# A 32-byte gap in on-chip memory ahead of the weights' pool of a two-layer hybrid encoder kernel

## The chip, the cores and the metric

The kernel runs on one core of a Trainium2 chip. The metric is the device time of one launch in microseconds (us). The kernel before takes 981.59 us, the median of three runs (981.29 to 983.07). Inside a core, TensorE multiplies matrices, VectorE (DVE), ScalarE (ACT) and GpSimd (POOL) do elementwise work, and SyncE (SP), among others, issues transfers (DMA). All of them read operands from a memory of 128 partitions (SBUF). A tile has the same byte address in each of its partitions, and this address is what the change moves.

## The reference

The kernel computes two layers of a bidirectional encoder for 256 positions and 2048 channels. Cut to what matters:

```python
for i in range(DEPTH):                       # DEPTH = 2
    hn = _rmsnorm(h, norm_g[i])
    u = hn @ w_in[i]                         # 2048 x 5632
    a_val, a_glu, a_z, q, k, v, b_z = jnp.split(u, offs, axis=-1)
    ya = _conformer_conv(a_val, a_glu, conv_w[i], conv_b[i], cln_g[i], cln_b[i])
    ya = ya * jax.nn.silu(a_z)
    yb = _window_attention(q, k, v, bias_band, sink[i]) * jax.nn.silu(b_z)
    h = h + jnp.concatenate([ya, yb], axis=-1) @ w_out[i]
    e = _rmsnorm(p[i] @ w_pe[i], pe_g[i])    # 256 x 2048
    h = h + e * jax.nn.sigmoid(h @ w_pg[i])
return _rmsnorm(h, final_g)
```

Everything is 32-bit floating point. Nearly all of the arithmetic lies in the products with `w_in`, `w_out`, `w_pg` and `w_pe`.

## The kernel before

**The products.** Activations lie transposed: channels on the partitions, the 256 positions along the free axis. A product has a block of weights of 128 x 128 as the stationary operand, which TensorE loads first (a weight load, PEld in the profile), and a block of activations, 128 x 256, as the moving operand, which then streams through (PE). To keep precision at a faster matmul type (`float32r`), each operand is split into a high and a low part, and a product is made of three: high times high, high times low, low times high. `mm3` does this in one of two forms. The narrow form (lines 402, 403, 404) issues three matmuls of 256 columns, each with its own weight load. The wide form (lines 399, 400) issues one matmul of 512 columns (high weights against the high and the low activations side by side), and one of 256 columns (low weights against the high activations), so two weight loads for the same 768 columns. The wide form is used for `w_pg` (tiles `g`) and half of `w_out` (tiles `o` with operand `ya`); the narrow one for everything else.

**The weights.** They arrive in transfers of 1 MB (tiles `raw`, pool `wraw`, three buffers), each holding two halves of 128 x 1024. For each half, `split` writes a tile `w` of pool `wspl` (five buffers): ScalarE casts the high part (line 166), VectorE subtracts it from the raw values for the low part (line 169). A half serves eight products. `get` and `ahead` make the split run up to four halves ahead of TensorE. The order on TensorE, VectorE and ScalarE is that in which the program is written: the scheduler is off for these three. Convolution steps on VectorE (line 577) are fed in between from a queue, a few for each half.

**Stages.** In each layer: `e` (`w_pe`), `ag` (convolution inputs), `k`, `v`, `zb` and `q` with attention in between, `za`, `o` (output projection), `g` (gate). In layer 0, `e` is made from `raw` without a split (line 499); in layer 1, it uses `w` against a small tile `pp`.

**Where the tiles lie.** Pools are laid out one behind the other in the order in which they are opened, and each tile takes a multiple of 32 bytes. The five pools of SBUF start at these byte addresses (in every partition), and the last column is the address modulo 64:

| pool, what it holds | size | start before | mod 64 |
|---|---|---|---|
| `big`: `hg`, `ya`, `yb`, `h` and other operands and sums | 5 x 16384 | 16512 | 0 |
| `wraw`: `raw` | 3 x 8192 | 98432 | 0 |
| `wspl`: `w` | 5 x 8192 | 123008 | 0 |
| `cst`: gains, parameters, `ident`, `ones`, then `mhalf` | 12064 | 163968 | 0 |
| ... of these, `keys` and all behind `mhalf` | | | 32 |
| `wk`: `pp`, `qq`, `sq`, `hn`, `s`, `ptt`, `v` and other working tiles | | 176032 | 32 |

`mhalf` needs 8 bytes and takes 32; hence what follows it, the whole pool `wk` except a few tiles of some bytes among it, lies half a line of 64 bytes off. Inside the tiles, the weight blocks of 128 columns lie 512 bytes apart, and the activations' blocks 1024, so that a matmul's operands start where their tile starts, modulo 64. So before the change `w` and the operands `hg`, `ya`, `yb`, `h` agree modulo 64, and three kinds of matmul have other pairs: `e` of layer 1 (moving `pp` at 32, weights `w` at 0), the attention scores `sc` (moving `keys` at 32, weights `qq` at 32), and the matmuls that multiply unsplit f32.

Of the kernel before, what the change touches and what calls it, by code (L numbers as in the profile page):

```python
# [10 lines left out]
F32 = mybir.dt.float32  # L11
# [6 lines left out]
P = 128  # L18
# [110 lines left out]
def trunk_kernel(ctx: ExitStack, tc: tile.TileContext, xT, pT, wst, par, gain, relb, sinkp, onehot, out):  # L129
    nc = tc.nc  # L130
# [2 lines left out]
        ctx.enter_context(tc.manual_schedule(engines={getattr(ET, x) for x in MAN.split(",")}))  # L133
    big = ctx.enter_context(tc.tile_pool(name="big", bufs=5))
    wraw = ctx.enter_context(tc.tile_pool(name="wraw", bufs=3))
    wspl = ctx.enter_context(tc.tile_pool(name="wspl", bufs=NSPL))
    cst = ctx.enter_context(tc.tile_pool(name="cst", bufs=1))
    wk = ctx.enter_context(tc.tile_pool(name="wk", bufs=2))
# [805 lines left out]
```

## Time and profile before

| what | value |
|---|---|
| median of three runs | 981.59 us |
| the profiled execution's span, first to last instruction | 978.2 us |
| mean granted TensorE clock | 0.997 |
| matmuls, weight loads | 7216, 7216 |
| HBM read and written, over the span | 185 GB/s |

The page gives no time of the profiled execution but its span, which is 3.4 us less than the median of the three runs. How to read it: PE is a matmul in flight and PEld a weight load in flight. Matmuls overlap, since one starts before the one ahead of it has left the array, so the busy share of PE says little. What tells the rate is the distance from the start of one matmul to the start of the next. A row of the timeline has a start, a duration, the engine, the source line, the operation, and output<-moving,stationary by the program's names.

### The profile page before, as it was taken

The page shows a single profiled execution, that of the slowest core. Times are in us where ns is not written, and L with a number is a line of the kernel's source. Part 1 is how long each engine was busy: PE and PEld are TensorE (multiplying, and loading weights), DVE is VectorE, ACT ScalarE, POOL GpSimd, SP SyncE. Part 2 cuts the span into 40 slices and gives each one's busy share as a digit, 9 for nine tenths or more (in the row PEclk, how much of TensorE's full clock was granted, in tenths as well). Part 3 has the DMA queues.
Part 4 walks back from the last instruction along what each step waited for, and adds up shares of the span by engine and source line. Part 5 has one row for each costly group of instructions (what it writes and reads, how often), then busy time and mean ns, then how long its engine had stood idle before and what let it go on. Part 6 is the DMA issues. An engine that isn't in the chain of part 4 may idle for free.

```text
span 978.2 us, 17740 instructions
## 1 busy us (share of the span) xinstructions
PE 965.9 (99%) x7216; PEld 914.6 (93%) x7216; DVE 793.7 (81%) x1369; ACT 557.9 (57%) x861; POOL 84.3 (9%) x79
## 2 busy tenths in 40 slices
PE   9999999999999999999999999999999999999996
PEld 7999999999999998888899999999999999888885
DVE  4899989987787777787789998988887878677763
ACT  4655455777774544555566444468787545446652
POOL 0022001010000000011103200000100000000111
PEclk9999999999999999999999999999999999999998
DMA  7664636555547454656546565565444555545532
GB/s 291 227 233 172 216 129 237 187 180 178 173 150 245 141 209 172 211 173 224 205 174 216 173 214 175 172 210 193 158 162 172 172 196 183 186 167 196 177 125 86
DMA packets 29005, 182.45 MB, mean 187 GB/s; under 512 B 3595, under 2 KB 4156, under 8 KB 9084
## 3 DMA queue, kind: packets, MB, share of 16 engines
q1 hardware_dynamic: 24284, 165.70, 48.6%
q0 software_dynamic: 3344, 12.88, 4.0%
q10 hardware_dynamic: 1296, 2.75, 0.8%
q8 instruction: 56, 0.92, 0.4%
q14 instruction: 25, 0.20, 0.1%
HBM read 177.09 MB, written 4.23 MB: 185 GB/s over the span
## 4 chain that ended last, share of the span: by engine, by line
PE 96%; DVE 2%; DMA 1%; ACT 0%; issue 0%; ACTq 0%; DVEq 0%
PE g L399 12%; PE o L399 6%; PE ag L404 6%; PE ag L402 6%; PE ag L403 6%; PE g L400 6%; PE za L402 3%; PE zb L402 3%; PE q L402 3%; PE o L402 3%; PE o L403 3%; PE o L404 3%; PE zb L403 3%; PE q L403 3%; PE za L403 3%; PE zb L404 3%
## 5 line engine op out<-in xcount | busy, mean ns | idle before, releaser
L169 DVE TENSOR_TENSOR w<-raw,w 128x1024 fp32r<-128x1024 f32 x306 | 372.3, 1226 | 104.9 <-ACT w L166 99.8
L166 ACT CAST w<-raw 128x1024 fp32r<-128x1024 f32 x308 | 314.2, 1046 | 161.2 <-PE ag L404 43.5
L577 DVE SCALAR_TENSOR_TENSOR cz<-az,pars,cz 128x241 f32<-128x241 f32 (+11 forms) x480 | 217.9, 503 | 1.9 <-ACT cz L570 0.9
L399 PE MATMUL g<-h,w 128*128 128x512 f32 x496 | 175.3, 399 | 0.0
L404 PE MATMUL ag<-hg,w 128*128 128x256 f32 x512 | 145.1, 283 | 0.5 <-DVE w L169 0.5
L402 PE MATMUL ag<-hg,w 128*128 128x256 f32 x512 | 145.4, 284 | 0.0
L403 PE MATMUL ag<-hg,w 128*128 128x256 f32 x512 | 145.0, 283 | 0.0
L400 PE MATMUL g<-h,w 128*128 128x256 f32 x496 | 139.3, 281 | 0.0
L399 PEld LDWEIGHTS g<-h,w 128*128 128x128 f32 x496 | 93.2, 188 | 23.2
L402 PEld LDWEIGHTS ag<-hg,w 128*128 128x128 f32 x512 | 97.5, 191 | 0.9 <-ACT cz L570 0.8
L404 PEld LDWEIGHTS ag<-hg,w 128*128 128x128 f32 x512 | 97.5, 191 | 0.8 <-DVE w L169 0.7
L403 PEld LDWEIGHTS ag<-hg,w 128*128 128x128 f32 x512 | 97.6, 191 | 0.1
L400 PEld LDWEIGHTS g<-h,w 128*128 128x128 f32 x496 | 93.7, 189 | 0.0
L399 PE MATMUL o<-ya,w 128*128 128x512 f32 x256 | 90.5, 399 | 0.0
L402 PE MATMUL za<-hg,w 128*128 128x256 f32 x256 | 73.7, 288 | 0.0
L402 PE MATMUL q<-hg,w 128*128 128x256 f32 x256 | 73.3, 286 | 0.0
L402 PE MATMUL zb<-hg,w 128*128 128x256 f32 x256 | 73.1, 286 | 0.0
L402 PE MATMUL o<-yb,w 128*128 128x256 f32 x256 | 73.1, 286 | 0.0
L403 PE MATMUL o<-yb,w 128*128 128x256 f32 x256 | 72.6, 283 | 0.0
L403 PE MATMUL zb<-hg,w 128*128 128x256 f32 x256 | 72.4, 283 | 0.0
L404 PE MATMUL o<-yb,w 128*128 128x256 f32 x256 | 72.4, 283 | 0.0
L403 PE MATMUL q<-hg,w 128*128 128x256 f32 x256 | 72.4, 283 | 0.0
(224 smaller groups left out, 2094.3 us busy)
## 6 DMA issues: line engine op xcount, KB each, us to landing
raw<-in_wst SPq DMA_DIRECT2D x153, 1024.0 KB, 4.9
bias<-fscr POOLq DMA_DIRECT2D x16, 384.0 KB, 3.7
raw<-in_wst SPq DMA_DIRECT2D x4, 512.0 KB, 8.1
az<-in_xT POOLq DMA_DIRECT2D x4, 512.0 KB, 6.0
hscr<-e POOLq DMA_DIRECT2D x2, 1024.0 KB, 5.0
az<-hscr POOLq DMA_DIRECT2D x4, 512.0 KB, 5.8
x<-in_xT SPq DMA_DIRECT2D x3, 512.0 KB, 8.3
out_t<-og ACTq DMA_DIRECT2D x4, 256.0 KB, 3.3
```

Of the source, the lines that this page charges most:

```text
L166: nc.scalar.copy(hi, raw)
L169: nc.vector.tensor_sub(lo, raw, hi.bitcast(F32))
L399: nc.tensor.matmul(o, w[:, 0], x, start=start, stop=False, skip_group_check=True)
L400: nc.tensor.matmul(o[:, 1], w[:, 1], x[:, 0], start=False, stop=stop, skip_group_check=True)
L402: nc.tensor.matmul(o, w[:, 0], x[:, 0], start=start, stop=False, skip_group_check=True)
L403: nc.tensor.matmul(o, w[:, 0], x[:, 1], start=False, stop=False, skip_group_check=True)
L404: nc.tensor.matmul(o, w[:, 1], x[:, 0], start=False, stop=stop, skip_group_check=True)
L577: nc.vector.scalar_tensor_tensor(acc[:, t, lo_:hi_], a[:, t, lo_ + s:hi_ + s], w(k), acc[:, t, lo_:hi_], ALU.mult, ALU.add)
```

## The change

A pool of one tile of 32 bytes is opened between `wraw` and `wspl`, and VectorE sets it to zero once.

```diff
     big = ctx.enter_context(tc.tile_pool(name="big", bufs=5))
     wraw = ctx.enter_context(tc.tile_pool(name="wraw", bufs=3))
+    gap = ctx.enter_context(tc.tile_pool(name="gap", bufs=1))
+    nc.vector.memset(gap.tile([P, 8], F32, name="gap"), 0.0)
     wspl = ctx.enter_context(tc.tile_pool(name="wspl", bufs=NSPL))
     cst = ctx.enter_context(tc.tile_pool(name="cst", bufs=1))
     wk = ctx.enter_context(tc.tile_pool(name="wk", bufs=2))
```

The addresses after it: `big` and `raw` stay. `w` starts at 123040, 32 modulo 64. The first part of `cst` is at 32, `keys` at 0, and `wk` starts at 176064, 0 modulo 64. So `w` differs by half a line from `hg`, `ya`, `yb`, `h`, and from `pp` too, with the sides exchanged (weights at 32, moving at 0). `qq` and `keys` agree as before, now at 0.

Of the instructions, one is added, and none is moved. At the program's start, VectorE's rows before were these (`zeros` is what the warming matmuls read, `relt` holds the bias table):

```order
L256 MEMSET zeros 128x256
L305 MEMSET ones 128x128
L307 MEMSET mhalf 128x2
L310 MEMSET relt 1x16
L389 TENSOR_TENSOR hacc<-hacc,sq 128x512 x6
```

and the same place of the changed kernel, where source lines stand two further down, has the row of the gap ahead of them:

```order
L137 MEMSET gap 128x8
L258 MEMSET zeros 128x256
L307 MEMSET ones 128x128
L309 MEMSET mhalf 128x2
L312 MEMSET relt 1x16
L391 TENSOR_TENSOR hacc<-hacc,sq 128x512 x6
```

Only this memset has moved the others down by one place. The rows of the other engines are the same ones in the same order.

## The prediction

> **What bounds the kernel now.** I read the page's shares first, then the chain of work that ended last, then TensorE's waits.
>
> ```profile
> PE 965.9 (99%) x7216; PEld 914.6 (93%) x7216; DVE 793.7 (81%) x1369; ACT 557.9 (57%) x861; POOL 84.3 (9%) x79
> ...
> PEclk9999999999999999999999999999999999999998
> ...
> PE 96%; DVE 2%; DMA 1%; ACT 0%; issue 0%; ACTq 0%; DVEq 0%
> ...
> PE rh0c L352 <- DVE fold L376: 1.2, 1, 1.2
> PE warm L259 <- DVE zeros L256: 1.2, 1, 1.2
> PE ag L404 <- DVE w L169: 0.5, 1, 0.5
> PE rfc L352 <- ACT sq L812: 0.4, 1, 0.4
> ```
>
> TensorE makes 96% of the chain, its granted clock is full, and by the last four rows (total, times, longest) it waits for other engines 3.3 us in all. Thus the span is the number of matmuls times the distance from one start to the next, and only what changes this distance moves the time. I take the distance from timeline rows. The first pair is the narrow form on `w` and `hg`, both at 0 modulo 64; the second is `e` of layer 1, the same form and the same engine order, with `w` at 0 and `pp` at 32.
>
> ```profile
> 299.78 0.28 PE L402 MATMUL za<-hg,w 128*128 128x256 f32 x1
> ...
> 301.94 0.28 PE L402 MATMUL za<-hg,w 128*128 128x256 f32 x1
> ...
> 497.51 0.28 PE L404 MATMUL e<-pp,w 128*128 128x256 f32 x1
> ...
> 501.38 0.28 PE L404 MATMUL e<-pp,w 128*128 128x256 f32 x1
> ```
>
> Between the first two lie 18 starts: 2.16 us / 18 = 120.0 ns. Between the other two lie 33: 3.87 / 33 = 117.3 ns. The groups by form say the same over all matmuls of these kinds, in their mean durations, and they add the weight loads:
>
> ```profile
> L404 PE MATMUL v<-w,hg 128*128 128x256 f32 x64 | 18.1, 283 | 0.0
> L403 PE MATMUL e<-pp,w 128*128 128x256 f32 x32 | 9.0, 280 | 0.0
> ...
> L404 PEld LDWEIGHTS za<-hg,w x256: 187/192/192, 249.2 to 779.6; 128*128 128x128 f32 x128
> L404 PEld LDWEIGHTS e<-pp,w x32: 187/188/192, 489.0 to 501.3; 128*128 128x128 f32 x32
> ```
>
> A matmul takes 283 ns where the two operands agree modulo 64 and 280 where they differ by half a line; in `v` the sides are exchanged (weights `hg`, moving `w`), and it is 283 all the same. A load's median is 192 ns and 188 ns (minimum/median/maximum). So the kernel before holds an example of what the change makes of all its products, and there a narrow matmul is 120.0 - 117.3 = 2.7 ns shorter.
>
> **The change, part by part.** *How many matmuls.* Seven rows of the groups on the page carry the counts:
>
> ```profile
> L399 PE MATMUL g<-h,w 128*128 128x512 f32 x496 | 175.3, 399 | 0.0
> L404 PE MATMUL ag<-hg,w 128*128 128x256 f32 x512 | 145.1, 283 | 0.5 <-DVE w L169 0.5
> L399 PE MATMUL o<-ya,w 128*128 128x512 f32 x256 | 90.5, 399 | 0.0
> L402 PE MATMUL za<-hg,w 128*128 128x256 f32 x256 | 73.7, 288 | 0.0
> L402 PE MATMUL q<-hg,w 128*128 128x256 f32 x256 | 73.3, 286 | 0.0
> L402 PE MATMUL zb<-hg,w 128*128 128x256 f32 x256 | 73.1, 286 | 0.0
> L402 PE MATMUL o<-yb,w 128*128 128x256 f32 x256 | 73.1, 286 | 0.0
> ...
> L402 PE MATMUL k<-hg,w 128*128 128x256 f32 x64 | 18.2, 284 | 0.0
> ...
> L402 PE MATMUL g<-h,w 128*128 128x256 f32 x16 | 4.5, 283 | 0.0
> ```
>
> Each line of the narrow form stands for three (402, 403, 404): 3 x (512 + 4 x 256 + 2 x 64 for `k` and `v` + 16) = 5040. The wide form has 496 + 256 = 752 pairs. At 120 ns the narrow ones are 604.8 us of the span.
>
> *Narrow form:* 5040 x 2.7 ns = 13.6 us, less what is not at 120 today. Behind each interruption some matmuls come closer together:
>
> ```profile
> 171.02 0.28 PE L645 MATMUL sc<-keys0h,qq 128*128 128x256 f32 x1
> ...
> 171.97 0.28 PE L402 MATMUL zb<-hg,w 128*128 128x256 f32 x1
> ...
> 172.32 0.28 PE L402 MATMUL zb<-hg,w 128*128 128x256 f32 x1
> ```
>
> After the scores (`sc`, eight of them in 0.95 us, 118.8 ns each), three `zb` take 0.35 us, 117 ns each, where `zb` is otherwise at 120. I estimate some 60 interruptions (48 of them by attention: scores, transposes and products for 16 pairs of heads), with some six such matmuls each, that have about 2 ns less to give: 0.7 us. The narrow form gives 12.9 us.
>
> *Wide form.* No row shows it with operands half a line apart; this is the unknown cost. Today three pairs take 1.06 us, 353.3 ns each:
>
> ```profile
> 419.98 0.40 PE L399 MATMUL g<-h,w 128*128 128x512 f32 x1
> 420.21 0.28 PE L400 MATMUL g<-h,w 128*128 128x256 f32 x1
> ...
> 421.04 0.40 PE L399 MATMUL g<-h,w 128*128 128x512 f32 x1
> ```
>
> Say that 256 columns cost c and a load that runs beside them s. Narrow, c + s = 120.0; wide, 3c + 2s = 353.3. So c = 113.3 ns and s = 6.7 ns. By this split `e` pays 4.0 ns for a load where its neighbours pay 6.7. I take the same 2.7 ns off each load, since `e` is the nearest row: 752 x 2 x 2.7 = 4.1 us. The ends are nothing at all, and a load that costs nothing, 752 x 2 x 6.7 = 10.1 us. A loss is not excluded either; it is a rival below.
>
> *The memset.* It stands ahead of `zeros` on VectorE, which the warming matmuls wait for.
>
> ```profile
> 0.86 0.27 DVE L256 MEMSET zeros<- 128x256 f32 x1 [0.86 <-PEq L933]
> ...
> 1.23 0.06 DVE L307 MEMSET mhalf<- 128x2 f32 x1
> ...
> 1.66 8.80 DMA x<-in_xT
> ```
>
> A memset of that size (`mhalf`) takes 0.06 us. The chain starts with the transfer of `x` (last row), so 0.06 us is hidden beneath 8.80 us; without that cover it would cost 0.06.
>
> *VectorE and ScalarE.* They write `w`, and most of their working tiles move by 32 bytes. Rows of the same operation and shape with different pairs before the change:
>
> ```profile
> L475 DVE TENSOR_TENSOR hg<-hn,hg 128x512 fp32r<-128x512 f32 x16 | 11.0, 686 | 0.5
> ...
> L806 DVE TENSOR_TENSOR e<-e,sg 128x512 f32<-128x512 f32 x14 | 9.7, 693 | 1.9 <-ACT sg L804 1.3
> ...
> L756 DVE TENSOR_TENSOR yb<-az,yb 128x512 fp32r<-128x512 f32 x8 | 5.2, 686 | 2.2 <-ACT yb L755 2.2
> ...
> L389 DVE TENSOR_TENSOR vacc<-vacc,sq 128x512 f32<-128x512 f32 x6 | 4.2, 692 | 4.3 <-ACT sq L388 4.3
> ```
>
> `yb` has all at 0 (686 ns), `hg` reads one at 32 (686), `e` reads one at 32 (693), `vacc` has all at 32 (692). No order by address: I cost this at nothing.
>
> *Is the weights' split fast enough?* VectorE is full in one stage. The first row is a stretch of the run with the busy time of PE, PEld, VectorE and ScalarE (and the instructions); the second is VectorE on line 169 alone, the third PE and PEld on line 404 alone, from other stretches.
>
> ```profile
> 60.00:120.00 60.00, 60.00 (x503) 60.00 (x502) 59.63 (x96) 28.39 (x36) 13.24 (x9) 1.00 0.57 193
> ...
> 0.00:95.00 95.00, 30.70 (x25) 1.00 0.67 237
> ...
> 24.00:95.00 71.00, 54.16 (x191) 36.63 (x191) 1.00 0.62 217
> ```
>
> In 60 to 120 us VectorE is busy 59.63 us, and TensorE waits all the same nowhere in it, since the split runs ahead. By 95 us, line 169 has run 25 times (second row), and line 174 twice: 27 halves; TensorE has started 191 third products (line 404, third row), eight a half, 23.9 halves. The lead is three halves or 3 x 24 x 120 ns = 8.6 us. TensorE faster by 2.2% eats 71 x 2.2% = 1.6 us of it by then. The cover holds. At the start of the first `ag`, where the wait of 0.5 us is, some tenths may come back: 0.3 us.
>
> **Sum:** 12.9 + 4.1 - 0.3 = 16.7 us off the span of 978.2, so 961.5. With the 3.4 us by which the median of the runs lies above this span, 981.6 - 16.7 = 964.9, say **965 us**, 1.7% less.
>
> One rule speaks against all of it. The Trainium skill, page "SBUF — State Buffer", section "SBUF: two separate sides", says that TensorE never waits for another user of the memory, and its section "A bandwidth-pool intuition that's wrong (but worth ruling out)" gives the weight load a second, independent read port. By that rule, a load and a stream could not disturb each other by their addresses, and the time would stay; 117.3 beside 120.0 ns is a first row against it.
>
> **The rivals.**
>
> *It does nothing.* The shorter distance in `e` could come from `pp` itself: it starts at 32, or lies far from `hg`, and its high and low parts are 2 KB apart where those of `hg` are 8 KB apart. Then `w` at 32 changes nothing; only `v`, whose moving operand is now `w` at 32, would gain 192 x 2.7 ns = 0.5 us, and `e` would lose 96 x 2.7 = 0.3. For it: the scores have both operands at 32, agree modulo 64, and still have 118.8 ns, not 120. Against it: they are only eight at a time, and behind an interruption `zb` shows such distances with both at 0. Time: 981.4, within 0.2%. The rule of the Trainium skill above ends here too.
>
> *Weights that begin in mid-line cost more (slower).* 512 bytes from a start at 0 are eight lines of 64; from 32 they touch nine. If what a load costs goes by its lines, and not by its relation to the stream, each load goes from 6.7 to 6.7 x 9/8 = 7.5 ns: 0.83 x (5040 + 1504) = 5.4 us, 987 us. It decides wherever the ninth line costs more than the half line saves. For it: no example has weights at 32 with a long run; `e` has the moving operand there. Against it: `qq` is a weight at 32, and the scores are not above 120.
>
> *The loads become free (much faster).* 6544 x 6.7 ns = 43.8 us, 938 us. For it is only that no conflict would be left in a simple picture of two half lines; `e`, which pays 4.0 ns for its loads, speaks against it.
>
> *Narrow only:* the wide form keeps 353.3 ns: 965 + 4.1 = 969, inside the forecast's own range.
>
> **How the numbers follow.** The forecast, 955 to 972 us, has a chance of 0.62; its upper end is a narrow form that gains only three quarters, with the wide unchanged, its lower end a free load in the wide form and some more in the narrow. Faster still, below 952: 0.05. A smaller gain, 972 to 979: 0.08. Nothing (a difference within 0.2%, about what a measurement of this kernel can tell from no change): 0.14. Slower: 0.11. So faster is 0.62 + 0.05 + 0.08 = 0.75, same 0.14, slower 0.11. The range that leaves out only the slower case and the loads that become nearly free reaches from 952 to 982.
>
> **What would show it.** Right: `za`, `zb`, `q`, `ag` at 280 ns a matmul and 188 a load instead of 283 and 192, eighteen starts in 2.11 us instead of 2.16; `g` with three pairs in about 1.044 instead of 1.06; `e` of layer 1 still at 117.3; VectorE's groups above with the same means; TensorE's waits still some 3 us. Wrong: 283 throughout with `v` alone at 280 (it was the moving operand's own start); 284 and more with `v` at 280 (weights in mid-line); distances that fall while TensorE's waits on `w` grow by as much (the split bounds); or a granted clock below 0.99.

## The result, and the profile after

The changed kernel takes 972.96 us (median of four runs, 972.3 to 973.9) beside 981.44 us of the kernel before. The ratio is 0.9914, with a 95% interval of 0.9899 to 0.9928. The gain is 8.5 us, where 16.7 were forecast: the sign and the place were right, and half of the size is missing. The time lies 1 us above the forecast range of 955 to 972 us, in the band of 972 to 979 that had been given a chance of 0.08.

The page of the changed kernel, with busy times, granted clock and the chain's shares:

```profile
PE 958.8 (99%) x7216; PEld 906.8 (93%) x7216; DVE 793.8 (82%) x1370; ACT 558.9 (57%) x861; POOL 81.0 (8%) x79
...
PEclk9999999999999999999999999999999999999999
...
PE 96%; DVE 2%; DMA 1%; ACT 0%; issue 0%; ACTq 0%; DVEq 0%
```

The shares are those of before: TensorE still sets the time. Its distances are read as before, from rows of the timeline a known number of starts apart. The first two rows are the narrow form, 30 starts apart; the other two are the wide form, twelve pairs apart:

```profile
296.67 0.28 PE L406 MATMUL za<-hg,w 128*128 128x256 f32 x1
...
300.21 0.28 PE L406 MATMUL za<-hg,w 128*128 128x256 f32 x1
...
403.44 0.40 PE L401 MATMUL g<-h,w 128*128 128x512 f32 x1
...
407.68 0.40 PE L401 MATMUL g<-h,w 128*128 128x512 f32 x1
```

Narrow: 3.54 us / 30 = 118.0 ns by these rounded rows (118.2 from the unrounded starts of the trace, which also give the later means; other stretches of 30 have up to 118.5). Wide: 4.24 us / 12 = 353.3 ns a pair. So the narrow form lost 1.8 of its 120.0 ns where 2.7 were expected, and the wide form lost nothing. The groups of loads and matmuls, with minimum/median/maximum in ns:

```profile
L406 PEld LDWEIGHTS za<-hg,w x256: 187/188/192, 248.2 to 774.0; 128*128 128x128 f32 x128
L406 PE MATMUL za<-hg,w x256: 276/280/288, 248.3 to 774.1; 128*128 128x256 f32 x128
L406 PEld LDWEIGHTS v<-w,hg x64: 187/188/189, 131.3 to 613.6; 128*128 128x128 f32 x64
L406 PE MATMUL v<-w,hg x64: 274/279/281, 131.4 to 613.7; 128*128 128x256 f32 x64
```

These medians, 188 and 280, are exactly the forecast's sign of success, and still the distance is not 117.3. The signs that were distances did not appear: eighteen narrow starts take 2.13 us (2.11 forecast), and three wide pairs still take 1.06 us (1.044 forecast). Before the change, the starts were evenly 120 ns apart. Now they repeat in an uneven pattern (116, 116, 120, 117, 122 and so on), and the durations that the profile gives have the same median, 280 ns, at this distance and in `e` before the change, at 117.3. The sign was badly chosen: a distance over many starts is safe, a median is not.

Where the 8.5 us came from is seen by taking the same work in both runs, from about the first `ag` matmul to the end, in stretches of the run (engines: PE, PEld, DVE, ACT, POOL). The first row is of the kernel before:

```profile
24.00:978.20 954.20, 944.29 (x7125) 896.21 (x7123) 783.96 (x1351) 546.89 (x844) 82.86 (x72) 1.00 0.53 184
```

and this is the changed kernel:

```profile
26.00:972.10 946.10, 936.20 (x7124) 888.07 (x7122) 783.72 (x1350) 547.80 (x844) 79.56 (x72) 1.00 0.53 185
```

The same number of matmuls but one takes 954.2 us before and 946.1 now: 8.1 us less, which is 5040 narrow matmuls times 1.6 ns (the mean over all of them fell from 119.9 to 118.3). The work of VectorE and ScalarE did not shrink or grow. The spans of the two profiled executions differ by 6.1 us only, since the changed one lost some 2 us in its first 26 us: there the granted clock was 0.79 between 17 and 25 us, and eight `e` matmuls took nearly twice as long, 3.62 us beside 1.97 before.

```profile
18.34 3.62 PE L501 MATMUL e<-p,raw 128*128 128x256 f32 x8
...
17.00:25.00 8.00, 8.00 (x37) 6.94 (x38) 3.90 (x6) 4.27 (x7) 0.70 (x1) 0.79 0.45 163
```

This dip is not of the change: another execution of the changed kernel has a mean clock of 0.998 and a span of 970.5 us, the profiled one 0.996 and 972.1; and a variant that is as slow as the kernel before (a gap of 256 bytes, below) has the dip too.

TensorE's waits on `w` did not grow. All its waits together went from 3.3 to 4.2 us (total, times, longest), by a later `rh0c` and a wait of `e` on a transfer, both in the first 17 us:

```profile
PE rh0c L354 <- DVE fold L378: 1.7, 1, 1.7
PE warm L261 <- DVE zeros L258: 1.2, 1, 1.2
PE ag L406 <- DVE w L171: 0.5, 1, 0.5
PE e L501 <- DMA raw<-in_wst: 0.4, 1, 0.4
PE rfc L354 <- ACT sq L814: 0.4, 1, 0.4
```

### The profile page after: what moved, and what is told of

Its sections match the earlier page's. It is cut to its first block, busy times and chain, and to the rows that moved or that the text cites. A ratio compares the mean times of both kernels' runs of the same rounds, so it can differ in the third digit from the quotient of the medians.

```text
span 972.1 us, 17741 instructions
## 1 busy us (share of the span) xinstructions
PE 958.8 (99%) x7216; PEld 906.8 (93%) x7216; DVE 793.8 (82%) x1370; ACT 558.9 (57%) x861; POOL 81.0 (8%) x79
## 4 chain that ended last, share of the span: by engine, by line
PE 96%; DVE 2%; DMA 1%; ACT 0%; issue 0%; ACTq 0%; DVEq 0%
PE g L401 12%; PE o L401 6%; PE g L402 6%; PE ag L406 6%; PE ag L404 6%; PE ag L405 6%; PE za L404 3%; PE q L404 3%; PE zb L404 3%; PE o L404 3%; PE o L402 3%; PE o L405 3%; PE o L406 3%; PE za L405 3%; PE q L405 3%; PE zb L405 3%
## 5 line engine op out<-in xcount | busy, mean ns | idle before, releaser
L171 DVE TENSOR_TENSOR w<-raw,w 128x1024 fp32r<-128x1024 f32 x306 | 374.0, 1232 | 101.1 <-ACT w L168 95.5
L406 PEld LDWEIGHTS ag<-hg,w 128*128 128x128 f32 x512 | 96.5, 188 | 0.9 <-DVE w L171 0.9
L404 PEld LDWEIGHTS ag<-hg,w 128*128 128x128 f32 x512 | 96.5, 188 | 0.9 <-ACT w L168 0.8
L405 PEld LDWEIGHTS ag<-hg,w 128*128 128x128 f32 x512 | 96.5, 188 | 0.1
L404 PE MATMUL zb<-hg,w 128*128 128x256 f32 x256 | 72.6, 284 | 0.0
L402 PE MATMUL o<-ya,w 128*128 128x256 f32 x256 | 72.1, 281 | 0.0
```

What stands on the lines that cost most here:

```text
L171: nc.vector.tensor_sub(lo, raw, hi.bitcast(F32))
L402: nc.tensor.matmul(o[:, 1], w[:, 1], x[:, 0], start=False, stop=stop, skip_group_check=True)
L404: nc.tensor.matmul(o, w[:, 0], x[:, 0], start=start, stop=False, skip_group_check=True)
L405: nc.tensor.matmul(o, w[:, 0], x[:, 1], start=False, stop=False, skip_group_check=True)
L406: nc.tensor.matmul(o, w[:, 1], x[:, 0], start=False, stop=stop, skip_group_check=True)
```

## The experiments

Most of them move tiles by gaps made like the one of the change: a pool of one tile, set to zero once. The last two, `lo64` and `mixed`, also move parts inside the tiles `w`. Everything else stays. It will help to have one name: **d**, the start of the weights (the stationary operand) minus the start of the moving operand. Blocks of weights lie 512 bytes apart and blocks of activations 1024, so d is the same for all products of a kind modulo 512 (in `lo64` and `mixed`, modulo 256).

**Relation or own start.** The first four kernels ask whether the two operands' relation counts or each one's own start, whether the shift of the other tiles has a part, and whether a gap as such does anything.

`x32` moves the operands and leaves `w` at its remainder modulo 64:

```diff
+    gap_big = ctx.enter_context(tc.tile_pool(name="gap_big", bufs=1))
+    nc.vector.memset(gap_big.tile([P, 8], F32, name="gap_big"), 0.0)
     big = ctx.enter_context(tc.tile_pool(name="big", bufs=5))
+    gap_wraw = ctx.enter_context(tc.tile_pool(name="gap_wraw", bufs=1))
+    nc.vector.memset(gap_wraw.tile([P, 8], F32, name="gap_wraw"), 0.0)
     wraw = ctx.enter_context(tc.tile_pool(name="wraw", bufs=3))
```

> Operands hg, ya, yb, h (pool big) moved to 32 modulo 64; w, raw, cst and wk keep the remainders of the kernel before. Theory R, only the relation of the two addresses counts: narrow matmuls as in the change, 118.2 ns apart, wide pairs 353.2; about 973 us. Theory S, each operand's own start counts, the moving one's more: narrow 116.7 to 117.3 ns as v and e have it with the moving operand at 32, v itself 118.2; 966 to 969 us if the wide form gains nothing, less if it does.

Measured: 973.69 us, ratio 0.9923 (0.9911 to 0.9935). Its narrow form:

```profile
296.65 0.28 PE L408 MATMUL za<-hg,w 128*128 128x256 f32 x1
...
300.19 0.28 PE L408 MATMUL za<-hg,w 128*128 128x256 f32 x1
```

3.54 us / 30 again, as in the change: the number of theory R.

`w32_x32` has four gaps of 32 bytes, ahead of `big`, `wraw`, `wspl` and `cst`:

> Both w and the operands of pool big at 32 modulo 64, all else with the remainders of the kernel before. Theory R: they agree again, narrow 120 ns, 981 us as before. Theory S: both gains add up, narrow some 115 ns, below 965 us.

Measured: 961.65 us, ratio 0.9811 (0.9792 to 0.9829). This is far from the 981 of theory R, and would fit theory S, had `x32` not spoken against it. Its narrow form comes down to this (30 starts):

```profile
291.69 0.28 PE L412 MATMUL za<-hg,w 128*128 128x256 f32 x1
...
295.09 0.28 PE L412 MATMUL za<-hg,w 128*128 128x256 f32 x1
```

3.40 us / 30 = 113.3 ns; other stretches have 117.8.

`w32_only` is the change with one more gap of 32 bytes, ahead of `cst`:

> The change with a second gap of 32 bytes behind the weights' pool, so that cst and wk keep the remainders of the kernel before and w alone differs. If the operands of the products make the whole gain: narrow 118.2 ns, 973 us. If the shift of the working tiles has a part in it: nearer to 981 us.

Measured: 972.7 us, ratio 0.9923 (0.9911 to 0.9936), narrow 118.2 ns. The working tiles are back at their old remainders modulo 64 (though 64 bytes further on), and the gain stays: their shift by half of that had no part that shows.

`gap64` has one gap, of 64 bytes, where the change has 32:

```diff
-    nc.vector.memset(gap.tile([P, 8], F32, name="gap"), 0.0)
+    nc.vector.memset(gap.tile([P, 16], F32, name="gap"), 0.0)
```

> A gap of 64 bytes in place of 32 ahead of the weights' pool: all remainders modulo 64 as before. Theories R and S: narrow 120 ns, 981 us. If the absolute place or the distance of the pools counts, or the added memset: another time.

Measured: 961.35 us, ratio 0.9798 (0.9784 to 0.9812). Both theories fall: all remainders modulo 64 are those of the slow kernel, and it is the fastest of the four. Its timeline has the narrow form at two distances. The first two rows are 30 starts apart, the second two as well:

```profile
153.82 0.28 PE L406 MATMUL q<-hg,w 128*128 128x256 f32 x1
...
157.22 0.28 PE L406 MATMUL q<-hg,w 128*128 128x256 f32 x1
...
289.76 0.28 PE L406 MATMUL za<-hg,w 128*128 128x256 f32 x1
...
293.30 0.28 PE L406 MATMUL za<-hg,w 128*128 128x256 f32 x1
```

3.40 / 30 = 113.3 ns in one stretch, 3.54 / 30 = 118 (117.8 from the unrounded starts) in the other. A stretch keeps its distance until the next interruption by attention or by a normalization, or until a product with another d follows (`zb` behind `v` goes from 117.8 to 113.3), and may have the other one behind it.

What makes one theory of all four is d, by the real differences of the addresses: 32 in the change and in `w32_only`, 64 - 32 = 32 in `x32`, 96 - 32 = 64 in `w32_x32`, and 64 in `gap64`. Equal d gives nearly equal times, wherever the operands start: 973, 973, 974 at 32 and 962, 961 at 64. So the relation counts, but not modulo 64. At 64 some luck is in it, since the two kernels do not have the two distances in the same stretches: `zb` has a mean of 114.0 ns in `gap64` and 116.8 in `w32_x32`, `ag` has 117.2 and 113.9.

**The period.** The next kernels use one gap of 96, 128, 192 or 256 bytes ahead of the weights' pool; `gapm32` has 32 bytes ahead of `big` and 480 ahead of `wraw`.

> A gap of 96 bytes ahead of the weights' pool. Theory D: what counts is the start of the weights minus the start of the moving operand, taken modulo 512, the size of a weight block, and not modulo 64. Call it d: 0 before (120.0 ns), 32 in the change (118.3), 64 with a gap of 64 (113.3, at times 117.8), and e of layer 1 before has d = 96 with 117.3. By D, narrow 117.3 ns, wide 353.3, about 967 us. If only modulo 64 counts (32 or 0): as the change, 973 us.

Measured: 967.53 us, ratio 0.9868 (0.9854 to 0.9883). Narrow (30 starts) and wide (twelve pairs):

```profile
296.00 0.28 PE L406 MATMUL za<-hg,w 128*128 128x256 f32 x1
...
299.52 0.28 PE L406 MATMUL za<-hg,w 128*128 128x256 f32 x1
...
401.50 0.39 PE L401 MATMUL g<-h,w 128*128 128x512 f32 x1
...
405.66 0.39 PE L401 MATMUL g<-h,w 128*128 128x512 f32 x1
```

117.3 ns as expected of `e`, and a wide pair now has 4.16 / 12 = 346.7 ns, 6.7 less. The expectation had left the wide form at 353.3; it is the first kernel in which it moved. But here too the narrow form has two distances: other stretches, most of those around attention in layer 0 among them, have 118.7, and the narrow mean is 117.8. In `v`, where the sides are exchanged, d is -96, or 160 modulo 256, and the distance is 120.0.

> A gap of 128 bytes ahead of the weights' pool, d = 128. If the memory repeats every 128 bytes: narrow 120.0 ns as with d = 0, 980 us. If it repeats later: another distance, nearer to the 113.3 or 117.8 ns of d = 64; the few scores (d = 128 before, eight at a time) say 119. Wide 353.3 either way, as in all runs so far.

Measured: 973.61 us, ratio 0.9929 (0.9915 to 0.9944): narrow 118.7, wide 351.1 ns. The narrow form, 30 starts:

```profile
296.98 0.28 PE L406 MATMUL za<-hg,w 128*128 128x256 f32 x1
...
300.54 0.28 PE L406 MATMUL za<-hg,w 128*128 128x256 f32 x1
```

A period of 128 bytes is excluded. The scores of the kernel before, which also have d = 128, had 118.8 ns.

> A gap of 256 bytes ahead of the weights' pool, d = 256, the farthest that two blocks can be from each other. A period of 128 or 256: narrow 120.0 ns, 980 us. A period of 512 with a conflict only where both streams are near each other: the smallest distance, 113.3 ns, 948 us.

Measured: 981.11 us, ratio 0.9999 (0.999 to 1.0008). Narrow, 30 starts:

```profile
299.82 0.28 PE L406 MATMUL za<-hg,w 128*128 128x256 f32 x1
...
303.42 0.28 PE L406 MATMUL za<-hg,w 128*128 128x256 f32 x1
```

3.60 / 30 = 120.0 ns and 353.3 for the wide pairs: the kernel before, to the nanosecond. Since 128 differs, a period of 256 bytes fits; this run shows it at d = 0 alone, and `mixed` below at two more values. The gap as such and its memset cost nothing that shows.

> The operands of pool big 32 bytes on, everything behind them 512 bytes on, so that d = -32 (480 modulo 512). Theory D: as v in the change, which has d = -32: narrow 116.7 ns, 965 us. A period of 128 makes it equal to d = 96. If only the amount of the difference counts: as the change, 118.3 ns and 973 us.

Measured: 962.32 us, ratio 0.9812 (0.9796 to 0.9829). Narrow (30 starts) and wide (twelve pairs):

```profile
294.19 0.28 PE L408 MATMUL za<-hg,w 128*128 128x256 f32 x1
...
297.69 0.28 PE L408 MATMUL za<-hg,w 128*128 128x256 f32 x1
...
399.49 0.39 PE L403 MATMUL g<-h,w 128*128 128x512 f32 x1
...
403.65 0.39 PE L403 MATMUL g<-h,w 128*128 128x512 f32 x1
```

The narrow form has 116.7 ns in most of its long stretches, as `v` has it in the change, and 117.8 in some; `v` itself, which now has d = 32, has the 118.3 of the change. Wide pairs have 346.7. So the sign of d matters: 32 and -32 differ by 11 us, 5.0 of them in the wide form (752 x 6.7 ns).

This kernel also shows that d alone does not fix the distance. `e` of layer 1 has d = 96 here as in the kernel before, but its 33 starts from 490.05 to 494.01 us are 120.0 ns apart, where the kernel before has 117.3. Other kernels with `e` at 96 have means between these two. So d decides which distances can occur; what picks one of them for a stretch is not known.

> Gap of 192 bytes, d = 192, the same as -64 by a period of 256. v has this pair with the gap of 64 bytes and 117.8 ns. Theory D with a period of 256: narrow 117.8 ns, 11 us less; wide not seen yet, 346.7 to 353.3; 965 to 971 us. If only the amount counts: as the gap of 64, 961 us.

Measured: 966.08 us, ratio 0.9839 (0.9826 to 0.9853): inside the expected range, though not by the expected distance alone. Its narrow form has the same two distances as `gap64`, 113.3 in the longest stretch of `ag` and in `v`, 117.8 in `za` and most others; the wide pairs stayed at 353.3. Two starts 60 matmuls apart in `ag`:

```profile
71.38 0.28 PE L404 MATMUL ag<-hg,w 128*128 128x256 f32 x1
...
78.17 0.28 PE L404 MATMUL ag<-hg,w 128*128 128x256 f32 x1
```

6.79 us / 60 is 113.2 ns by these rounded rows. It is 5 us slower than `gap64`; some 3 of them come from which stretches have which distance (a narrow mean of 116.7 beside 116.1 ns). Since the distances themselves are the same, this run does not tell whether the sign matters at 64.

All kernels with one d, sorted by d modulo 256 (two values: the long stretches of one kernel have one or the other; `v` and `e` are left out):

| d | kernels | narrow, ns | wide pair, ns | us |
|---|---|---|---|---|
| 0 | before, `gap256` | 120.0 | 353.3 | 980 to 982, 981.11 |
| 32 | the change, `x32`, `w32_only` | 118.2 to 118.5 | 353.3 | 972.96, 973.69, 972.7 |
| 64 | `gap64`, `w32_x32` | 113.3 or 117.8 | 353.3 | 961.35, 961.65 |
| 96 | `gap96` | 117.3 or 118.7 | 346.7 | 967.53 |
| 128 | `gap128` | 118.7 | 351.1 | 973.61 |
| 192 | `gap192` | 113.3 or 117.8 | 353.3 | 966.08 |
| 224 | `gapm32` | 116.7 or 117.8 | 346.7 | 962.32 |

**Which load disturbs which stream.** `lo64` has no gap; it moves the low half inside each tile `w`, which grows by 256 bytes so that all buffers keep one remainder modulo 256:

```diff
-        w = wspl.tile([P, 2, HALF], F32R, tag="w", name=f"w{h}")
+        w = wspl.tile([P, 2 * HALF + 64], F32R, tag="w", name=f"w{h}")
+        w = w[:, 0:2 * HALF + 32].rearrange("p (a b) -> p a b", a=2)[:, :, 0:HALF]
```

> No gap; inside each tile w the low part lies 64 bytes further, so that d = 0 for the loads of high parts and 64 for those of low parts. Theory: a load disturbs the stream that runs beside it, so only the matmul ahead of each low part's load (line 403 of the kernel before) changes, 120 to between 113.3 and 117.8 ns, the other two of three stay at 120: mean 117.8 to 119.3, 970 to 978 us. If it is the place of the whole tile that counts: 120 ns throughout, 981 us.

Measured: 967.03 us, ratio 0.9847 (0.9834 to 0.9861), faster than expected. The three matmuls of a product, in groups with mean ns (lines 403, 404, 405 here are 402, 403, 404 of before):

```profile
L403 PE MATMUL v<-w,hg 128*128 128x256 f32 x64 | 17.9, 279 | 0.0
L405 PE MATMUL v<-w,hg 128*128 128x256 f32 x64 | 17.9, 279 | 0.0
L404 PE MATMUL v<-w,hg 128*128 128x256 f32 x64 | 17.8, 278 | 0.0
```

The expectation failed in its detail: not one of three is shorter, all are, from 283 or 284 to 278 or 279 ns. The sum is telling: a narrow product takes 3 x 117.8 = 353.3 ns in place of 360, which is 6.7 ns less, as if one load of three had become free (120 + 120 + 113.3) and the saving were shared out. In the wide form the pair came to 346.7, again 6.7 less (twelve pairs, 4.16 us by the unrounded starts):

```profile
401.60 0.39 PE L400 MATMUL g<-h,w 128*128 128x512 f32 x1
...
405.75 0.39 PE L400 MATMUL g<-h,w 128*128 128x512 f32 x1
```

Part of the 967 us is that the wide form gained too, which the expectation had left out. A price that falls for every load as d goes from 0 to 64 does not explain it: with all loads at d = 64 (`gap64`) a wide pair gains nothing, and with the low ones alone at 64 it gains 6.7 ns. So which load disturbs which stream stays open.

**The best of both.** The table says that no single d is best for both forms. `mixed` has a gap of 64 bytes and writes the halves for the wide form 32 bytes further inside the tile:

```diff
-        w = wspl.tile([P, 2, HALF], F32R, tag="w", name=f"w{h}")
+        name, _, k0, _ = HALVES[h % NHALF]
+        o = 8 if name == "w_pg" or name == "w_out" and k0 == 0 else 0
+        w = wspl.tile([P, 2 * HALF + 64], F32R, tag="w", name=f"w{h}")
+        w = w[:, o:o + 2 * HALF].rearrange("p (a b) -> p a b", a=2)
```

> Gap of 64 bytes ahead of the weights' pool, and the halves that the wide form reads (w_pg, and w_out against ya) written 32 bytes further inside their tiles, which take 256 bytes more each so that all buffers keep one remainder modulo 256. So d = 64 for the narrow form and d = 96 for the wide one. Theory D with a period of 256: narrow 113.3 ns or 117.8 as with the gap of 64, wide pairs 346.7 ns in place of 353.3: 752 x 6.7 ns = 5.0 us less than the gap of 64, about 956 us. If the wide form's gain at 96 came from something else: 961 us.

Measured: 955.37 us (953.45 to 955.53), ratio 0.9720 (0.9707 to 0.9734). Its wide form, twelve pairs apart:

```profile
395.41 0.39 PE L404 MATMUL g<-h,w 128*128 128x512 f32 x1
...
399.57 0.39 PE L404 MATMUL g<-h,w 128*128 128x512 f32 x1
```

4.16 / 12 = 346.7, and the narrow form has its two distances as in `gap64`. The expectation held to within a microsecond: of the 6.0 us less than `gap64`, the wide pairs give 5.0, and about 1.0 comes, by the two traces, from `o` with `yb`, whose mean is 116.4 ns here and 117.7 there. Each form so keeps the distances of its own d. The run also supports the period: a tile of 8448 bytes is 16.5 times 512, so that from one buffer to the next d alternates between 96 and 352 in the wide form and between 64 and 320 in the narrow one, and the pairs have 346.7 ns in all buffers. This kernel beats the change by 18 us and the kernel before by 26.

## Why the prediction was half right

- *What bounds the kernel.* Right. Only the distance between matmuls changed, and the whole difference of 8.1 us over the same work is 5040 times its change.
- *"So the kernel before holds an example of what the change makes of all its products."* This step failed, and with it went the missing 8 us, about 4.8 in the narrow form and 4.1 in the wide one. `e` was taken as an example because it differs by half a line modulo 64. But `pp` lies at 198688 and `w` at 123008: modulo 256, the period that the runs showed, their starts are 32 and 128, so d = 96, while the change made d = 32. The two are alike modulo 64, and the kernels differ. `gap96`, which gives all products but `v` the d of `e`, has 117.3 ns in many stretches and 967.53 us, near the 965 that was forecast: the price read from `e` fits its own d, though 118.7 and 120.0 occur there too. That the direction came out right is in part luck: what the example shared with the change was only that d was no longer 0, and of the whole kernels tried, all but those with d = 0 and 256 are faster.
- *Narrow form, 12.9 us.* It gave 8.1 (5040 x 1.6 ns), for that reason.
- *Wide form, 4.1 us.* It gave nothing: 353.3 ns. The assumption that a load saves there what it saves in the narrow form has no support; at d = 64 the narrow form saves most and the wide form nothing, at 96 the wide form 6.7 ns a pair.
- *The split into c = 113.3 and s = 6.7 ns.* 113.3 came back as the shortest distance in any of these kernels, and 6.7 as the step of savings in `lo64` and in the wide form. That a load costs s beside any stream is not so: the shares differ by form and d.
- *Memset, VectorE, the split's lead.* Right. VectorE's line 169 (171 now) went from a mean of 1226 to 1232 ns, and TensorE's wait on the `w` that it writes is 0.5 us as before, even in kernels 20 us faster.

```profile
L171 DVE TENSOR_TENSOR w<-raw,w 128x1024 fp32r<-128x1024 f32 x306 | 374.0, 1232 | 101.1 <-ACT w L168 95.5
```

The 0.3 us set aside for the early `ag` were not needed.

- *The rivals.* "It does nothing" had the right doubt, that `pp` might be no example, but sought it in the moving operand's own start; `x32` and `w32_only`, equal to each other with different operands moved, exclude that. Its evidence, scores that agree modulo 64 and still have 118.8 ns, is explained by their d of 128. Weights in mid-line do not cost more: in `w32_x32` they start there, and it is among the fastest. Lines of 64 bytes, on which that rival and the talk of half a line rest, appear in no run: `gap64` keeps all remainders modulo 64 and is 19 us faster. Loads that are free by the forecast's split appear in part, at 113.3 ns.
- *The rule that stood against all of it.* The Trainium skill, page "SBUF — State Buffer", section "SBUF: two separate sides", has TensorE wait for nobody. Where it is taken to mean, as in the prediction, that TensorE's own loads and streams do not disturb each other, it is not borne out here: with the same matmuls in the same order, tiles that were moved by 64 bytes take the narrow form from 120.0 to 113.3 ns in some stretches and 117.8 in the others.

What is not settled: why 256 bytes are the period, why several distances are stable at one d, and what picks one of them. The runs show that the relation of the two addresses decides which distances occur; no run here shows the memory's inside. Nor was d = 160 tried for all products; `v` in `gap96` has it, at 120.0 ns.

## What to carry to other kernels

Where TensorE is the bound and its matmuls each load new weights, lay out the weights and the moving operands with a chosen difference of their start addresses, and measure a few differences up to 256 bytes: here it is worth up to 2% for one gap, and 2.8% with one difference for each form of product. An example in the old trace is only an example if all that could matter agrees: compare full addresses, not the remainder that the idea speaks of. And read a rate from the distance over many starts, since the median of the durations hides an uneven pattern.

## What the runs showed of the hardware

- The distance between narrow matmuls depends on the weights' start minus the moving operand's start, and on its sign: 120.0 ns at 0 and 256, 118.2 to 118.5 at 32, 116.7 or 117.8 at -32. A period of 256 bytes fits all runs, and one of 128 does not (118.7 at 128).
- At some differences there are several stable distances: 113.3 and 117.8 ns at 64 and 192; 117.3, 118.7 and, in `e` of one kernel, 120.0 at 96. Which one holds can change behind an interruption of the stream.
- A pair of the wide form took 353.3 ns at 0, 32, 64 and 192, 351.1 at 128 and 346.7 at 96 and -32.
- When a third of the loads had the better difference, the gain of 6.7 ns for each product was spread over all three of its matmuls.
- The times in which VectorE and ScalarE write `w` hardly moved with the tiles' addresses (means of 1226 to 1233 ns for the low parts and 1045 to 1048 for the high parts, over all thirteen kernels).
